# Local attention of both heads of a tile together, and three longer distances in the recurrence's order

## The chip, the cores and the metric

The kernel runs on one core of a Trainium2 chip. The metric is the device time of one execution in microseconds (us). In the text PE is TensorE (its weight loads are shown apart, as PEld), DVE is VectorE, ACT is ScalarE, POOL is GpSimd and SP is SyncE, which here only starts transfers. L517 is line 517 of the kernel.

## What is computed

One layer of a hybrid decoder for 256 prompt tokens and 8 samples of 8 tokens each, 320 columns in all, at model width 2048:

```
xn = RMSNorm(x);  p = xn @ w_in            # 82 tiles of 128 columns
A: RWKV-7 time mixing, 12 heads x 64: per token  S = S*w + sa (kk*a)^T + v k^T,  o = S r
B: sliding-window attention (window 128), 12 query heads on 4 key/value heads, 64 wide,
   softmax with a learned sink per head; the samples also see 128 cached keys each
C: cross-attention, 4 heads x 128, into 256 memory tokens
merged = sum_i sigmoid(gate_i) * (o_i @ w_br_i);  h = x + RMSNorm(merged @ w_o)
y = h + RMSNorm((gelu(conv3(z_gate)) * z_val) @ w_ffn_down)
```

All data are 32-bit floats. Branch B is what the change reorders, and in branch A three places of its order.

## The kernel before, in words

**The weight stream.** Every large product is made with split operands: a weight chunk of up to 8 tiles is loaded by SP, ACT rounds it to its upper part (`wh`, L356 or L96) and DVE subtracts to get the lower part (`wl`, L357 or L97); each weight tile then meets 320 columns in a group of three matmuls (L101 to L103). All activations are kept transposed, features on partitions and tokens in columns.

**The planner.** In the recurrence and the attention PE's order is written out while the program is built, by `pump`: a clock counts 0.405 for each group of three matmuls of the job queue; threads (Python generators) hand in their small operations between groups and give with `yield d` the distance until they go on, or a condition to wait for. PE runs exactly this order; the order on DVE, ACT and POOL is chosen by the tile framework's scheduler, and semaphores keep what depends on what. A distance that is too short shows as a wait on PE.

**The recurrence** (about 88 to 545 us) treats the 12 heads as 6 pairs `hp`. The job queue holds for each pair the projections k, r, v (16 groups each) and then 2 or 3 filler jobs (q, k, v of the attention, 16 groups each); after these come the 16 gate jobs. A job's `done` (L447 to L456) shifts the tokens of its result on POOL, ACT and DVE. `allearly` runs `early(hp)` for one pair after another; its places on PE are, in order:

- L493, the decay and a projections;
- 1.5 behind k: the scaled key `kk` and its square on ACT (L505, L506), and at once the norm matmul L517, which sums the squares; DVE follows with L518 to L524;
- behind r: `ar` and `bk` on DVE (L529 to L533), and 4.0 later the scores L543; here the thread `inverse(hp)` starts, whose first DVE operations (L620, L621) stand 6.0 later and need a round trip by DMA (`sc`, then `NI`);
- 2.0 later the transposes L566 and L572 (of `ar`), with copies by DVE and ACT (L578, L583);
- 1.5 behind v: the transposes of v, again L572, with eight copies into AU by DVE and ACT in turns (L593);
- `TRS` = 2.4 later the 20 products L600, their copy L601, and the bonus matmul L603.

`inverse(hp)` and `late(hp)` (the state's chain and the output) run as threads of their own, about one pair behind. The PSUM banks of `early` and of the tail of `late` come from one pool of two (`pea`).

**The attention** (about 550 to 800 us) runs two threads between groups of the remaining gate and branch jobs: one goes through the memory attention of the prompt (`mem_prompt`, 4 heads) and then through the 6 tiles of the local attention (`swa_prompt`), the other through the memory attention of the samples (`mem_sample`) and then their local attention (`swa_sample`, 2 tiles x 2 groups of 4 samples). A tile has two query heads, one on partitions 0 to 63, the other on 64 to 127. Before, they are done one after the other: scores (two matmuls, 64 rows by 128 columns of the array, 128 and 256 columns streamed), softmax on DVE and ACT (`sink_softmax`), `SSOFT` = 6.0 later three transposes (L869) and their copy (L872), `TRN` = 2.0 later the values (L985, L986: 128 rows by 64 columns). For the samples the scores of one head are four strips of 32 columns (L1005, L1007). Scores and transposes take their PSUM banks from a pool of 3 (`smp1`), the accumulators from a pool of 2 for the prompt and 1 for the samples (`accp`).

Of the kernel before, what the change touches and what calls it, by code (L numbers as in the profile page):

```python
# [9 lines left out]
F32 = mybir.dt.float32  # L10
# [4 lines left out]
PSUM = bass.MemoryType.PSUM  # L15

T = 320
TP = 256
# [11 lines left out]
E0 = 9.0  # L30
TRS = 2.4
NRM = (4, 3, 2)
# [6 lines left out]
SOFT = 3.5  # L39
SSOFT = 6.0  # L40
TRN = 2.0
# [21 lines left out]
def tile_hybrid_step(ctx: ExitStack, tc: tile.TileContext, i, o):  # L63
    nc = tc.nc
    V, A, G, PE = nc.vector, nc.scalar, nc.gpsimd, nc.tensor
# [84 lines left out]
    def split(h, l, src):  # L150
        A.copy(out=h, in_=src)  # L151
        V.tensor_sub(out=l, in0=src, in1=h.bitcast(F32))
# [10 lines left out]
    mv = ap.tile([128, 2, 512], F32, tag="mv", name="mv")  # L163
    QKV = ap.tile([128, 10, T], F32, tag="QKV", name="QKV")
# [3 lines left out]
    with tc.tile_pool(name="st", bufs=1, side="right") as st, tc.tile_pool(name="st2", bufs=3, side="right") as st2, \  # L168
# [122 lines left out]
        sm = spread(smp, smt, 1, tbs=TB[:2])  # L291
# [42 lines left out]
    clock = [0.0]  # L334
# [71 lines left out]
    with tc.tile_pool(name="rws", bufs=1, side="right") as rws, tc.tile_pool(name="rwp", bufs=2, side="right") as rwp, \  # L406
# [31 lines left out]
        def tt():  # L438
            return rwt.tile([128, T], F32, tag="t", name="rt")
# [47 lines left out]
        def early(hp):  # L487
# [17 lines left out]
            A.activation(out=kk, in_=sk, func=AF.Copy, scale=col("kk", hp))  # L505
            A.activation(out=sq, in_=kk, func=AF.Square)  # L506
            eLe, eL = x1, tt()
            A.activation(out=eLe, in_=x1, func=AF.Exp, scale=-C2)
            A.activation(out=eL, in_=L, func=AF.Exp, scale=-C2)
            emL = L  # L510
            A.activation(out=emL, in_=L, func=AF.Exp, scale=C2)
            yield lambda: state["late"] >= hp - 1
            pc = rwm.tile([128, 16], F32, tag="pc", name="pc")
# [72 lines left out]
            sv = rkv[hp, "v"]  # L586
            yield 1.5
            ps1 = pea.tile([128, 512], F32, tag="sm", name="sm")
            turned(ps1, sv)
            for q in range(4):  # L590
                for h in range(2):
                    ng = 3 if q < 2 else 2
                    (A.copy if h else V.tensor_copy)(out=AU[64 * h + 32:64 * h + 64, q:min(4 * ng, 10):4, 64:128],  # L593
                                                     in_=ps1[32 * q:32 * q + 32, 0:128 * ng].rearrange("p (g f) -> p g f", f=128)[:, :, fss[h]])
            yield TRS
            ps1 = pea.tile([128, 512], F32, tag="sm", name="sm").rearrange("p (c t) -> p c t", t=64)
# [217 lines left out]
    with tc.tile_pool(name="at", bufs=1, side="right") as at, tc.tile_pool(name="at2", bufs=2, side="right") as at2, \  # L814
            tc.tile_pool(name="smp1", bufs=3, space=PSUM) as smp, tc.tile_pool(name="accp", bufs=2, space=PSUM) as accp, \
            tc.manual_schedule(engines=MANUAL):
# [61 lines left out]
        def mem_unit(h, qb, pso):  # L878
            pss = smp.tile([128, 512], F32, tag="sm", name="sm")
            PE.matmul(pss[:, 0:256], MQ[:, h, 128 * qb:128 * qb + 128], mkT[:, h, :], start=True, stop=True)  # L880
            pr = softmax(pss[:, 0:256], 256, MS, "p")
            yield SOFT
            pt = transposed(pr, ((0, 128), (128, 128)), "p")
            yield TRN
            for kb in range(2):
                PE.matmul(pso[:, 128 * qb:128 * qb + 128], mv[:, kb, 128 * h:128 * h + 128],
                          pt[:, 128 * kb:128 * kb + 128], start=kb == 0, stop=kb == 1)

        def mem_prompt(h):
            pso = accp.tile([128, 512], F32, tag="acc", name="pso")  # L890
            for qb in range(2):
                yield from mem_unit(h, qb, pso)
            split(OMH[:, h, 0:TP], OML[:, h, 0:TP], pso[:, 0:TP])
            state["om"] += 1

        def mem_sample():
            for b in range(8):
                bg, s = b // 4, b % 4
                if s == 0:
                    po = accp.tile([128, 512], F32, tag="accs", name="psos", bufs=1)  # L900
                ck = at2.tile([128, 4, 256], F32, tag="ck", name="ck")
# [49 lines left out]
        def sink_softmax(src, mask, n, sinkcol, blocks, th):  # L951
# [16 lines left out]
            return pr  # L968

        def swa_prompt(ti):  # L970
            pso = accp.tile([128, 512], F32, tag="acc", name="pso")
            for r in range(2):
                rs = slice(64 * r, 64 * r + 64)
                n = 2 * (ti // 3) + r
                head = 3 * n + ti % 3
                kt = 6 + ti // 3
                pss = smp.tile([128, 512], F32, tag="sm", name="sm")
                PE.matmul(pss[:, 0:128], QKV[rs, ti, 0:128], QKV[rs, kt, 0:128], start=True, stop=True)
                PE.matmul(pss[:, 128:384], QKV[rs, ti, 128:256], QKV[rs, kt, 0:256], start=True, stop=True)
                pr = sink_softmax(pss[:, 0:384], amask[:, 0:384], 384, snk[:, head:head + 1], ((0, 128), (128, 384)), "p")  # L980
                yield SSOFT
                pt = transposed(pr, ((0, 128), (128, 128), (256, 128)), "p")
                yield TRN
                vd = slice(64 * n, 64 * n + 64)
                PE.matmul(pso[rs, 0:256], Vt[:, 0, vd], pt[:, 0:256], start=True, stop=False)  # L985
                PE.matmul(pso[rs, 128:256], Vt[:, 1, vd], pt[:, 256:384], start=False, stop=True)  # L986
            split(OSH[:, ti, 0:TP], OSL[:, ti, 0:TP], pso[:, 0:TP])
            state["os"] += 1

        def swa_sample(n2):  # L990
            for bg in range(2):
                po = accp.tile([128, 512], F32, tag="accs", name="psos", bufs=1)
                ck = at2.tile([128, 4, 128], F32, tag="ck", name="sck")
# [3 lines left out]
                yield 4.0  # L997
                for r in range(2):
                    rs = slice(64 * r, 64 * r + 64)
                    n = 2 * n2 + r  # L1000
                    pss = smp.tile([128, 512], F32, tag="sm", name="sm")
                    for s in range(4):
                        b = 4 * bg + s
                        q = QS[rs, n2, b, :]
                        PE.matmul(pss[32 * s:32 * s + 32, 0:128], q, ck[rs, s, :], start=True, stop=True,  # L1005
                                  tile_position=(64 * r, 32 * s))
                        PE.matmul(pss[32 * s:32 * s + 32, 128:192], q, QKV[rs, 6 + n2, TP:T], start=True, stop=True,  # L1007
                                  tile_position=(64 * r, 32 * s))
                    pr = sink_softmax(pss[:, 0:192], amask[:, 384 + 192 * bg:576 + 192 * bg], 192, snk[:, 12 + n:13 + n], ((0, 192),), "s")
                    yield SSOFT  # L1010
                    pt = transposed(pr, ((0, 128), (128, 64)), "s")
                    yield TRN
                    vd = slice(64 * r, 64 * r + 64)
                    PE.matmul(po[:, vd], pt[0:64, 128:256], Vn[:, 64 * n:64 * n + 64], start=True, stop=False)
                    for s in range(4):
                        PE.matmul(po[32 * s:32 * s + 32, vd], pt[:, 32 * s:32 * s + 32], cv[:, s, vd], start=False, stop=True,
                                  tile_position=(0, 32 * s))
                ob = at2.tile([128, 128], F32, tag="ob", name="ob")
# [340 lines left out]
```

## Time and profile before

| | |
|---|---|
| median of 3 runs | 2075.04 us (2074.26 to 2076.94) |
| profiled execution: its own time | 2076.5 us |
| profiled execution: span, first to last instruction | 2074.7 us |
| granted PE clock, mean over the span | 0.987 |
| busy: PE, DVE, ACT, POOL | 97%, 59%, 40%, 10% |
| memory traffic, mean | 146 GB/s |

The clock is that of PE in shares of full speed (2.4 GHz; the other level is 1.2 GHz, shown as 0.50). A matmul of 32-bit floats that are not rounded leaves two records. An "idle" time stands with what ended it: `[2.24 <-ACT rt L506]` means that the engine waited 2.24 us and that ACT's operation at L506 on tile `rt` released it. A span of a merged row is from the start of its first record to the end of its last.

### The profile page before, as it was taken

Reading aid. Unit: us, or ns where it says so; the run is one execution under the profiler, and the core shown is the slowest. Engines: PE = TensorE matmul, PEld = TensorE weight load, DVE = VectorE, ACT = ScalarE, POOL = GpSimd, SP = SyncE. Lnnn points to the kernel's source line nnn. Section 1 sums busy time; section 2 is a strip of 40 time slices with the busy share of each in tenths; the row PEclk is TensorE's granted clock in tenths of the full one; section 3 lists DMA queues with packets and bytes.
Section 4 is the critical chain, followed back from the end, with each engine's and each line's share of the span. In section 5 each row is a group of like instructions: output and inputs, shape, how many; then the busy total and the mean of one; then the engine's idle time right before and its main releaser. Section 6 shows DMA issues by size and latency. Waiting matters only on the chain.

```text
span 2074.7 us, 36358 instructions
## 1 busy us (share of the span) xinstructions
PE 2009.7 (97%) x14875; PEld 1940.3 (94%) x14875; DVE 1234.4 (59%) x2048; ACT 823.3 (40%) x1306; POOL 197.7 (10%) x452
## 2 busy tenths in 40 slices
PE   8899898989999999999999999999999999999997
PEld 7788797889998899999999999999999999999997
DVE  7778778885456764444546753555555555455456
ACT  5534343343333443333445443343333333334335
POOL 4511221021200000000100100000000000000001
PEclk9999899999999999999999999999999999999998
DMA  7443333334545334544543344445444444444444
GB/s 272 160 126 96 113 114 96 93 119 127 181 170 160 114 122 142 163 152 150 191 173 132 129 152 146 150 153 187 147 151 152 148 148 152 153 148 147 153 138 125
DMA packets 93000, 303.28 MB, mean 146 GB/s; under 512 B 11356, under 2 KB 17654, under 8 KB 92816
## 3 DMA queue, kind: packets, MB, share of 16 engines
q1 hardware_dynamic: 83232, 273.42, 39.7%
q0 software_dynamic: 8880, 26.71, 4.0%
q8 instruction: 117, 1.92, 0.4%
q10 hardware_dynamic: 720, 0.82, 0.1%
q14 instruction: 51, 0.42, 0.1%
HBM read 293.53 MB, written 9.34 MB: 146 GB/s over the span
## 4 chain that ended last, share of the span: by engine, by line
PE 84%; issue 6%; DVE 5%; DMA 2%; ACT 1%; POOL 1%; SPq 0%; POOLq 0%; DVEq 0%; ACTq 0%
PE bigps L101 25%; PE bigps L102 25%; PE bigps L103 24%; DMA NI<-sc 1%; DVE wl L357 1%; ACT wh L356 1%; DMA sc<-BT 0%; PE bigps L1130 0%; DVE wl L217 0%; PE sm L869 0%; PE sm L493 0%; PE bigps L1128 0%; PE bigps L1131 0%; PE sm L701 0%; PE sm L146 0%
## 5 line engine op out<-in xcount | busy, mean ns | idle before, releaser
L101 PE MATMUL bigps<-XH,wh 128*128 128x320 f32 x2656 | 846.3, 319 | 0.5 <-ACT mv L319 0.5
L103 PE MATMUL bigps<-XH,wl 128*128 128x320 f32 x2656 | 826.7, 311 | 2.1 <-DVE wl L357 2.1
L102 PE MATMUL bigps<-XL,wh 128*128 128x320 f32 x2656 | 827.0, 311 | 1.6 <-POOL XL L257 1.5
L101 PEld LDWEIGHTS bigps<-XH,wh 128*128 128x128 f32 x2656 | 504.5, 190 | 18.9 <-issue 14.8
L97 DVE TENSOR_TENSOR wl<-raw,wh 128x1024 fp32r<-128x1024 f32 (+1 forms) x299 | 357.4, 1196 | 274.7 <-ACT wh L96 273.9
L96 ACT CAST wh<-raw 128x1024 fp32r<-128x1024 f32 (+1 forms) x299 | 306.4, 1025 | 519.4 <-PE bigps L102 396.6
L102 PEld LDWEIGHTS bigps<-XL,wh 128*128 128x128 f32 x2656 | 504.5, 190 | 4.3 <-POOL XL L257 2.4
L103 PEld LDWEIGHTS bigps<-XH,wl 128*128 128x128 f32 x2656 | 503.9, 190 | 2.6 <-DVE wl L357 2.6
L357 DVE TENSOR_TENSOR wl<-raw,wh 128x1024 fp32r<-128x1024 f32 (+2 forms) x212 | 245.4, 1158 | 190.1 <-ACT wh L356 189.9
L356 ACT CAST wh<-raw 128x1024 fp32r<-128x1024 f32 (+2 forms) x212 | 208.4, 983 | 313.6 <-PE bigps L102 262.7
L102 PE MATMUL bigps<-fl,wh 128*128 128x320 f32 x704 | 217.5, 309 | 0.0
L101 PE MATMUL bigps<-fh,wh 128*128 128x320 f32 x704 | 217.4, 309 | 0.0
L103 PE MATMUL bigps<-fh,wl 128*128 128x320 f32 x704 | 217.4, 309 | 0.0
L101 PEld LDWEIGHTS bigps<-fh,wh 128*128 128x128 f32 x704 | 132.2, 188 | 0.2 <-ACT fh L151 0.2
L102 PEld LDWEIGHTS bigps<-fl,wh 128*128 128x128 f32 x704 | 132.2, 188 | 0.1
L103 PEld LDWEIGHTS bigps<-fh,wl 128*128 128x128 f32 x704 | 132.2, 188 | 0.0
L1187 DVE TENSOR_TENSOR yacc<-yacc,bigps 128x320 f32<-128x320 f32 x80 | 38.9, 487 | 84.4 <-PE bigps L103 84.2
L1161 POOL COPY cout<-zp 128x9 f32<-128x9 f32 x88 | 16.8, 221 | 732.4 <-DVE zp L1158 732.4
L101 PE MATMUL bigps<-MG,wh 128*128 128x320 f32 x208 | 64.4, 309 | 0.3 <-ACT MG L811 0.3
L103 PE MATMUL bigps<-MG,wl 128*128 128x320 f32 x208 | 64.3, 309 | 0.0
L102 PE MATMUL bigps<-MG,wh 128*128 128x320 f32 x208 | 64.3, 309 | 0.0
L1157 DVE TENSOR_TENSOR zp<-bigps,S 128x256 f32<-128x256 f32 x44 | 18.7, 425 | 57.1 <-PE bigps L103 57.1
(406 smaller groups left out, 2393.5 us busy)
## 6 DMA issues: line engine op xcount, KB each, us to landing
raw<-in_wup SPq DMA_DIRECT2D x176, 512.0 KB, 3.6
raw<-in_win SPq DMA_DIRECT2D x164, 512.0 KB, 3.6
raw<-in_wdn SPq DMA_DIRECT2D x80, 512.0 KB, 3.2
raw<-in_wo SPq DMA_DIRECT2D x32, 512.0 KB, 3.8
raw<-in_wbr_rw SPq DMA_DIRECT2D x16, 384.0 KB, 3.2
raw<-in_wbr_sw SPq DMA_DIRECT2D x16, 384.0 KB, 3.2
ck<-in_cmk POOLq DMA_DIRECT2D x8, 512.0 KB, 4.8
cv<-in_cmv POOLq DMA_DIRECT2D x8, 512.0 KB, 3.8
```

The source lines that it names most:

```text
L96: A.copy(out=h, in_=raw)
L97: V.tensor_sub(out=l, in0=raw, in1=h.bitcast(F32))
L101: PE.matmul(ps, h, xh, start=start, stop=False)
L102: PE.matmul(ps, h, xl, start=False, stop=False)
L103: PE.matmul(ps, l, xh, start=False, stop=stop)
L356: A.copy(out=h, in_=c[2])
L357: V.tensor_sub(out=l, in0=c[2], in1=h.bitcast(F32))
L1157: V.tensor_mul(out=zp[:, 2:258], in0=psz[:, 0:TP], in1=S2[:, 0:TP])
L1161: G.tensor_copy(out=cout[:, j, :, e], in_=zp[:, 256 + e:337 + e:10])
L1187: V.tensor_add(out=yacc[:, m, :], in0=yacc[:, m, :], in1=ps)
```

## The change

Three distances in `early`: the norm matmul stands at least `KKN` = 3.2 behind the operations on ACT that it needs (before: at once); the turning of v stands `TRN_V` = 3.6 behind v (before 1.5); the products stand `PRE` = 4.8 behind the turning (before 2.4).

In the local attention both heads of a tile are done together. For the prompt the scores of one head and block of keys are two matmuls of 64 query columns each in place of one of 128, issued so that they alternate between the four 64 x 64 quarters of the array; each head has its own PSUM bank. Then come both softmaxes, `SSOFT2` = 9.0 later the transposes of both, `TRN2` = 3.6 later the values of both, on the two column halves. For the samples the strips of both heads alternate in the same way, and the transposes and values of both stand together. `smp1` gets 4 banks, `accp` 1 and 1; the accumulator of the prompt is asked for just ahead of the first values matmul.

```
-TRS = 2.4
+KKN, TRN_V, PRE = 3.2, 3.6, 4.8
-SSOFT = 6.0
+SSOFT2, TRN2 = 9.0, 3.6
...
             A.activation(out=sq, in_=kk, func=AF.Square)
+            ready = clock[0] + KKN
...
-            yield lambda: state["late"] >= hp - 1
+            yield lambda: state["late"] >= hp - 1 and clock[0] >= ready
...
             sv = rkv[hp, "v"]
-            yield 1.5
+            yield TRN_V
...
-            yield TRS
+            yield PRE
...
-            tc.tile_pool(name="smp1", bufs=3, space=PSUM) as smp, tc.tile_pool(name="accp", bufs=2, space=PSUM) as accp, \
+            tc.tile_pool(name="smp1", bufs=4, space=PSUM) as smp, tc.tile_pool(name="accp", bufs=1, space=PSUM) as accp, \
...
         def swa_prompt(ti):
+            kt = 6 + ti // 3
+            pss = [smp.tile([128, 512], F32, tag="sm", name="sm") for _ in range(2)]
+            for lo, hi, q0, k1 in ((0, 128, 0, 128), (128, 384, 128, 256)):
+                for c in range(2):
+                    for r, rs in enumerate(halves2):
+                        qs = slice(64 * (c ^ r), 64 * (c ^ r) + 64)
+                        PE.matmul(pss[r][qs, lo:hi], QKV[rs, ti, q0 + qs.start:q0 + qs.stop], QKV[rs, kt, 0:k1], start=True, stop=True)
+            prs = []
+            for r in range(2):
+                head = 6 * (ti // 3) + 3 * r + ti % 3
+                prs.append(sink_softmax(pss[r][:, 0:384], amask[:, 0:384], 384, snk[:, head:head + 1], ((0, 128), (128, 384)), "p"))
+            yield SSOFT2
+            pts = [transposed(pr, ((0, 128), (128, 128), (256, 128)), "p") for pr in prs]
+            yield TRN2
             pso = accp.tile([128, 512], F32, tag="acc", name="pso")
...
+            for r, rs in enumerate(halves2):
+                PE.matmul(pso[rs, 0:256], Vt[:, 0, vd[r]], pts[r][:, 0:256], start=True, stop=False)
+            for r, rs in enumerate(halves2):
+                PE.matmul(pso[rs, 128:256], Vt[:, 1, vd[r]], pts[r][:, 256:384], start=False, stop=True)
...
         def swa_sample(n2):
...
+                pss = [smp.tile([128, 512], F32, tag="sm", name="sm") for _ in range(2)]
+                for s in range(4):
+                    for r, rs in enumerate(halves2):
+                        q = QS[rs, n2, 4 * bg + s, :]
+                        PE.matmul(pss[r][32 * s:32 * s + 32, 0:128], q, ck[rs, s, :], start=True, stop=True,
+                                  tile_position=(64 * r, 32 * s))
+                        PE.matmul(pss[r][32 * s:32 * s + 32, 128:192], q, QKV[rs, 6 + n2, TP:T], start=True, stop=True,
+                                  tile_position=(64 * r, 32 * s))
+                prs = [sink_softmax(pss[r][:, 0:192], ...) for r in range(2)]
+                yield SSOFT2
+                pts = [transposed(pr, ((0, 128), (128, 64)), "s") for pr in prs]
+                yield TRN2
...
```

## Rows read from the trace of the kernel before

**Rows 1.** The page, part 1: busy time of PE, share of the span and instructions.

```profile
PE 2009.7 (97%) x14875; PEld 1940.3 (94%) x14875; DVE 1234.4 (59%) x2048; ACT 823.3 (40%) x1306; POOL 197.7 (10%) x452
```

**Rows 2.** Windows by stage: length, PE, PEld, DVE, ACT, POOL busy, PE clock, DMA share, GB/s.

```profile
100.00:500.00 400.00, 367.91 (x3409) 336.21 (x3408) 309.73 (x568) 155.08 (x315) 72.38 (x140) 0.95 0.36 108
...
553.00:800.00 247.00, 246.37 (x1888) 222.81 (x1887) 154.71 (x384) 95.61 (x218) 18.17 (x33) 1.00 0.48 153
```

**Rows 3.** Waits of PE: total us, times, longest us.

```profile
PE sm L517 <- ACT rt L506: 10.6, 5, 2.3
PE sm L600 <- DVE AU L593: 9.7, 8, 1.8
PE sm L572 <- DVE rkv L454: 9.4, 6, 1.6
```

**Rows 4.** PE's timeline (start, length), two groups at each clock; one window.

```profile
252.00 0.47 PE L101 MATMUL bigps<-XH,wh 128*128 128x320 f32 x1
...
252.80 0.47 PE L101 MATMUL bigps<-XH,wh 128*128 128x320 f32 x1
...
254.89 0.31 PE L101 MATMUL bigps<-XH,wh 128*128 128x320 f32 x1
...
255.33 0.31 PE L101 MATMUL bigps<-XH,wh 128*128 128x320 f32 x1
...
244.00:255.00 11.00, 10.22 (x56) 8.06 (x57) 8.97 (x20) 2.37 (x5) 0.00 (x0) 0.53 0.15 48
```

**Rows 5.** PE's timeline, places of the first head pair.

```profile
97.83 0.81 PE L517 MATMUL sm<-rt,cst 128*128 128x320 f32 x2 [2.24 <-ACT rt L506]
...
108.24 1.38 PE L543 MATMUL sm<-ar,bk 64*64 64x64 f32 x40
...
116.67 0.78 PE L572 MATMUL sm<-cst,rkv 128*128 128x128 f32 x3 [1.58 <-DVE rkv L454]
...
123.19 0.92 PE L600 MATMUL sm<-AU,BT 32*32 32x64 f32 x28 [1.23 <-DVE AU L593]
```

**Rows 6.** DVE: a window, the splits L357 in it, the timeline's L532.

```profile
98.60:107.30 8.70, 8.38 (x14) 1.00 0.23 72
...
98.60:107.30 8.70, 2.44 (x2) 1.00 0.23 72
...
106.75 0.49 DVE L532 TENSOR_TENSOR ar<-rkv,rt 128x320 f32<-128x320 f32 x1
```

**Rows 7.** DVE's timeline among the copies into AU.

```profile
119.81 0.17 DVE L620 TENSOR_TENSOR prod<-rcst,NI 120x4 f32<-120x4 f32 x1 [1.14 <-DMA NI<-sc]
...
122.85 0.29 DVE L593 COPY AU<-sm 32x128 f32<-32x128 f32 x1
```

**Rows 8.** PE's timeline, one prompt head's values and the next scores.

```profile
631.51 0.31 PE L103 MATMUL bigps<-ORH,wl 128*128 128x320 f32 x1
631.75 0.65 PE L985 MATMUL pso<-pt,Vt 128*64 128x256 f32 x2
...
632.55 0.48 PE L978 MATMUL sm<-QKV 64*128 64x128 f32 x2
...
633.40 0.41 PE L101 MATMUL bigps<-ORH,wh 128*128 128x320 f32 x1
```

**Rows 9.** PE's timeline, one sample head's values and the next scores.

```profile
689.94 0.43 PE L1014 MATMUL psos<-Vn,pt 64*128 64x64 f32 x2
...
691.03 0.41 PE L101 MATMUL bigps<-OMH,wh 128*128 128x320 f32 x1
```

**Rows 10.** PE's timeline, four column strips of the memory attention's values.

```profile
577.93 0.64 PE L917 MATMUL psos<-cv,pt 128*32 128x128 f32 x16
578.50 0.71 PE L886 MATMUL pso<-pt,mv 128*128 128x128 f32 x4
```

**Rows 11.** DVE's timeline, first and last operation of one sample softmax.

```profile
691.72 0.35 DVE L953 TENSOR_TENSOR pr<-sm,amask 128x192 f32<-128x192 f32 x1
...
696.83 0.31 DVE L967 TENSOR_SCALAR pr<-pr,stat 128x192 f32<-128x192 f32 x1
```

More of the change, by code (lines that the diff above doesn't have):

```diff
@@ L884, in mem_unit @@
             yield TRN
+            if qb == 0:
+                pso.append(accp.tile([128, 512], F32, tag="acc", name="pso"))
             for kb in range(2):
-                PE.matmul(pso[:, 128 * qb:128 * qb + 128], mv[:, kb, 128 * h:128 * h + 128],
+                PE.matmul(pso[0][:, 128 * qb:128 * qb + 128], mv[:, kb, 128 * h:128 * h + 128],
                           pt[:, 128 * kb:128 * kb + 128], start=kb == 0, stop=kb == 1)
         def mem_prompt(h):
-            pso = accp.tile([128, 512], F32, tag="acc", name="pso")
+            pso = []
             for qb in range(2):
                 yield from mem_unit(h, qb, pso)
-            split(OMH[:, h, 0:TP], OML[:, h, 0:TP], pso[:, 0:TP])
+            split(OMH[:, h, 0:TP], OML[:, h, 0:TP], pso[0][:, 0:TP])
             state["om"] += 1
@@ L899, in mem_sample @@
                 if s == 0:
-                    po = accp.tile([128, 512], F32, tag="accs", name="psos", bufs=1)
+                    po = accp.tile([128, 512], F32, tag="accs", name="psos")
                 ck = at2.tile([128, 4, 256], F32, tag="ck", name="ck")
@@ L968, in sink_softmax @@
             return pr
+        halves2 = [slice(64 * r, 64 * r + 64) for r in range(2)]
         def swa_prompt(ti):
-            pso = accp.tile([128, 512], F32, tag="acc", name="pso")
[L972 to L986, printed above, removed]
+            kt = 6 + ti // 3
[12 more added lines that the diff above has]
+            yield TRN2
+            pso = accp.tile([128, 512], F32, tag="acc", name="pso")
+            vd = [slice(64 * (2 * (ti // 3) + r), 64 * (2 * (ti // 3) + r) + 64) for r in range(2)]
+            for r, rs in enumerate(halves2):
+                PE.matmul(pso[rs, 0:256], Vt[:, 0, vd[r]], pts[r][:, 0:256], start=True, stop=False)
+            for r, rs in enumerate(halves2):
+                PE.matmul(pso[rs, 128:256], Vt[:, 1, vd[r]], pts[r][:, 256:384], start=False, stop=True)
@@ L991, in swa_sample @@
             for bg in range(2):
-                po = accp.tile([128, 512], F32, tag="accs", name="psos", bufs=1)
+                po = accp.tile([128, 512], F32, tag="accs", name="psos")
                 ck = at2.tile([128, 4, 128], F32, tag="ck", name="sck")
@@ L997, in swa_sample @@
                 yield 4.0
[L998 to L1001, printed above, removed]
-                    for s in range(4):
[L1003 to L1017, printed above, removed]
@@ new lines, in swa_sample @@
+                prs = [sink_softmax(pss[r][:, 0:192], amask[:, 384 + 192 * bg:576 + 192 * bg], 192,
+                                    snk[:, 12 + 2 * n2 + r:13 + 2 * n2 + r], ((0, 192),), "s") for r in range(2)]
+                yield SSOFT2
+                pts = [transposed(pr, ((0, 128), (128, 64)), "s") for pr in prs]
+                yield TRN2
+                for r, rs in enumerate(halves2):
+                    PE.matmul(po[:, rs], pts[r][0:64, 128:256], Vn[:, 128 * n2 + 64 * r:128 * n2 + 64 * r + 64], start=r == 0, stop=False,
+                              skip_group_check=True)
@@ L1018, in swa_sample @@
+                for r, rs in enumerate(halves2):
+                    for s in range(4):
+                        PE.matmul(po[32 * s:32 * s + 32, rs], pts[r][:, 32 * s:32 * s + 32], cv[:, s, rs], start=False, stop=True,
+                                  tile_position=(0, 32 * s), skip_group_check=True)
                 ob = at2.tile([128, 128], F32, tag="ob", name="ob")
```

## The prediction, made before the changed kernel was run

> **What bounds the kernel now.** I read the page's busy shares first, then the windows by stage, then the list of waits of TensorE (PE), and last the timelines of PE and VectorE (DVE) around each wait.
>
> PE is busy for 97% of the span [rows 1], so the time is PE's work plus its gaps. The windows say where the gaps are: from 100 to 500 us (the recurrence) PE works 367.9 of 400 us at a mean granted clock of 0.95; from 553 to 800 us (the attention) it works 246.4 of 247 us at full clock [rows 2]. So the recurrence can be shortened by taking gaps away, and the attention only by giving PE less to do. The three largest waits there are the ones that the three distances concern: the norm matmul L517 behind the square on ScalarE (ACT), 10.6 us; the products L600 behind the copies into AU, 9.7 us; the turning of v, L572, behind its token shift, 9.4 us [rows 3]. Together 29.7 us.
>
> Part of the lost time is clock. At full clock one group of three matmuls of the weight stream takes 0.44 us, at the lower of the two levels 0.80 us [rows 4], so 45% of such time is lost. A mean clock of 0.95 over 400 us is 40 us at half clock [rows 2], worth at most 40 x 0.45 = 18 us (less, as some of it is waiting). The drop from 244 to 255 us follows the waits of one L600 [rows 4]; but after the 2.24 us wait for the first L517 [rows 5] the clock stayed at 1.00 [rows 6], so not every wait costs clock.
>
> **The change, part by part.** The planner's clock counts 0.405 per group, so a distance is a number of groups of 0.44 us: 1.5 is 4 groups, 2.4 is 6, 3.2 is 8, 3.6 is 9, 4.0 is 10, 4.8 is 12. Weight jobs are always there to fill them: after v come 2 or 3 filler jobs of 16 groups, and the longer path behind v takes 9 + 12 = 21 groups (before 4 + 6). So the distances themselves cost nothing; their order of work stays, and they issue no DMA.
>
> *Turning of v (1.5 to 3.6).* The first L572 on v stands at 116.67 us after 1.58 us of waiting and 4 groups (1.76 us) [rows 5]: v's last matmul was over at 113.33 and its shift was ready 3.34 us later. Nine groups are 3.96 us, 0.6 us to spare, in all six head pairs alike. Gain 9.4 us; I take 9, bounds 6 (if the shift is late behind a weight split on DVE) and 9.4.
>
> *Norm matmul (KKN).* k was over at 97.83 - 2.24 - 1.76 = 93.83 us; the square is ready 4.0 us later [rows 5], and the new place, 4 + 8 = 12 groups behind k, is 5.3 us later. L517's wait goes. But what is late next is the scores matmul L543. It keeps its place, 10 groups behind r, and r is 16 groups behind k: with about 0.7 of the norm matmul's own 0.81 us that is 26 x 0.44 + 0.7 = 12.1 us after k, at 105.9. From L517's start to the end of L532, the last DVE operation that the scores need, it is 107.24 - 97.83 = 9.4 us, and DVE worked 8.4 of 8.7 us there, two weight splits of together 2.4 us among it [rows 6]. Started at 99.1 this chain ends at 108.5, or at 107.3 if one of the two splits now falls ahead of it. The wait of 2.24 us comes back as one of 1.4 to 2.6 us in front of the scores. In the later head pairs the tail of the pair before adds DVE work and some PE work to the same stretch. Bounds for the six together: 10.6 us gained (DVE's order changes so that the chain fits) to 5 lost (2.6 six times). I take a gain of 3, about the lower wait in each pair.
>
> *Products (TRS 2.4 to PRE 4.8).* L600's last inputs came at 123.19 us, 9.86 us behind v [rows 5]; 21 groups and the turning's 0.55 us put it at 9.8. If the copies stayed where they are, the wait would be gone. They do not quite: they come from the turning, now 0.6 us later, and DVE runs in order. Already before, the copies stood in DVE's queue behind L620, which waited 1.14 us for the DMA that brings NI; the last DVE copy was issued at 122.85, 3.0 us after it [rows 7]. With the copies issued later, more of them fall behind that DMA. So between nothing gained and all 9.7; I take 5, as half of each wait is then covered.
>
> *Clock.* With some 17 of 30 us of waits gone I take 8 of the 18 us; bounds 0 and 18.
>
> *Prompt attention.* For one head PE now runs L985, L986 (values) and then L978, L979 (scores of the next head). The last weight matmul starts at 631.51 and takes 0.15, the next starts at 633.40: 1.74 us per head, of which the scores are 0.85 and the values 0.80 [rows 8]. Two heads per tile make 3.48 us. In the change the values of both heads stand on two column halves next to each other, and the scores on four quarters. If those run at once, a tile costs what a head did: gain 6 x 1.74 = 10.4 us. That halves run at once the trace shows: the 20 scores matmuls of the recurrence, each of 64 columns on one of two diagonal quarters, take 1.38 us [rows 5], while at 0.85 us per 384 columns in a row they would be 2.8. Four quarters at once, two of them in the same columns, stand nowhere in the trace. Bounds for the scores: 0.85 per tile (four at once), 1.70 (two at once, as now), 3.40 (one by one).
>
> *Column halves that share all rows* are the one point where a page speaks against the change. The row: eight matmuls on four column strips, all 128 rows, take 0.57 us until the next group starts [rows 10]; by the 0.85 us per 384 columns they would be 2.3 us in a row. The Trainium skill, "TensorE: Matmul & The Clock Gate", Part 3, "The mechanism", says that a weight load overlaps matmuls in flight only where the row group differs; by that the value halves would run in turn. The trace disagrees by a factor of four, so I keep the gain, and give the rule a small chance below.
>
> *Sample attention.* One head takes from about 689.85 to 691.03, 1.18 us [rows 9], 8 heads. Together, the scores of two (0.48 us, eight strips) may cost one, the two L1014 then stand next to each other, and L1016 gains nothing (both heads on the same strips): about 0.8 us per pair, 3.3 us in all; bounds 0 and 4.7.
>
> *Waits in the attention.* The distances per pair (9.0 and 3.6: 23 and 9 groups, 10.1 and 4.0 us) replace two of 6.0 and 2.0. One sample unit took from 691.72 to 697.14 between its first and last DVE operation while the other thread's unit ran too [rows 11]. The second head runs behind the first on DVE and ACT, so a pair needs between 5.4 and 10.8 us; nearest to the lower end plus one unit's own DVE work (some 2.5 us), 8 us, inside 10.1. I set 1.7 us aside for waits, so the attention gives 10.4 + 3.3 - 1.7 = 12 us. The single accumulator bank is asked for only at the values, 12.6 clock units after the last split, and costs nothing.
>
> **Sum** against the profiled execution (2076.5 us, span 2074.7): 9 + 3 + 5 + 8 + 12 = 37 us less, 2039.5. That execution lies 1.5 us above the median of the runs shown (2075.0), so the forecast is 2038.
>
> **Rivals.**
> *The waits form again on DVE* (25%). For it: 8.4 of 8.7 us in rows 6, and the queue in rows 7. Against it: one of the two splits can fall ahead of L517. L572's 9 and the attention's 12 stay, L600 gives 0, the norm loses 3 (2.3 in each pair), the clock nothing: 18 us less, 2057.
> *All waits and all slow clock go* (12%). For it: the covers counted in groups suffice at L572 and L600. Against it: the scores' chain. 14 + 30 + 18 = 62 us less, 2013.
> *The quarters do not run four at once* (8%), so that the change does not do what it says. Nothing in the trace has two row halves in the same columns together. Two at once: 0.85 x 6 + 0.48 x 4 = 7 us of the gain go, 2045; one by one: another 10, 2055.
> *Column halves in turn* (3%): 0.80 x 6 = 4.8 us of the gain go, 2043. This is what the rule of "TensorE: Matmul & The Clock Gate" in the Trainium skill gives here; rows 10 speak against it.
> *The pair's softmax is late at the transposes L869: slower than before* (6%). If both chains run one after the other at 5.4 us and are held up by the splits, 10.8 us and more meet 10.1. What such a wait costs in clock is open: none after the 2.24 us before the first L517, but 11 us x 0.47 x 2 x 0.45 = 4.6 us from 244 on, behind a wait of at most 1.8 us [rows 3, 4]; half of that is 2.3. There are 10 pairs; to eat 37 us each must lose 3.7 us, that is a wait of 1.4 us with its clock. At 2 us it is 10 x 4.3 = 43: 2081. Against it: L869 is not among the large waits now [rows 3], and DVE is 63% busy there (154.7 of 247 us) [rows 2]. The Trainium skill, "TensorEngine Tiling (Array Packing)", "PSUM Bottleneck", states the same danger: tiling speeds up TensorE and not the engines that empty PSUM; no run yet shows it here.
>
> **How the numbers follow.** Forecast 46%, with its own range 2026 to 2052. The range 2014 to 2062 takes in the second, fourth and fifth cases and half of the third; about 2 in 10 is left out, on the low side of "all go", on the slower side, and in sums of the bounds. A difference of 0.2% (4 us) is about what a measurement can tell. Faster by more: 0.91 (everything but the slow rival and sums of bad bounds); within: 0.04; slower: 0.05.
>
> **What would show it.** In the trace of the changed kernel: L572 without waits; L517 without, and L543 with waits of 1 to 2.5 us behind DVE; L600 with waits under 1 us; PE's clock from 100 to 460 us above 0.96; the gap in the weight stream at a tile's values and the next one's scores 1.7 to 1.9 us, once per tile, and the waits at L869 under 0.5 us each. The forecast is wrong if the quarters take over 1.3 us per tile, if L543 stays free of waits and the clock at 1.00, or if L869 waits by microseconds.

## The result, and the profile of the changed kernel

The changed kernel takes 2053.36 us (median of 4 runs, 2050.91 to 2054.78) against 2075.99 us (4 runs of the kernel before beside it): a ratio of 0.9886, 95% interval 0.9871 to 0.9902, some 23 us less. The forecast was 2038, its range 2014 to 2062: faster as forecast, by about 60% of the amount. The profiled execution took 2050.9 us, 25.6 less than that of before.

Below, the recurrence is the stretch on PE from the first L493 to the last matmul of `late` (L763 before, L764 after); what follows it holds the gates, the attention and the feed-forward. The change moves most lines of the recurrence by one (L517 is now L518, L543 L544, L572 L573, L600 L601) and the local attention's further (scores L982, values L993 and L995, transposes L870).

| profiled execution | before | after | forecast |
|---|---|---|---|
| recurrence, us | 460.3 | 448.0 (-12.3) | -25 |
| from there to the end, us | 1525.5 | 1512.4 (-13.1) | -12 |
| waits of PE in the recurrence, us | 33.8 | 28.5 | -17 |
| half-clock time in it, us | 41.0 | 41.0 | clock gains 8 |

(Half-clock time is (1 - granted clock) x 2, summed over windows of 1 us.) The profiled execution of after is the shortest of its four, so the timed difference of 23 us is the safer one. The attention gave what was asked and the recurrence about half.

The page's part 1 of after, and its two windows by stage, to set beside [rows 1, 2]:

```profile
PE 1988.0 (97%) x14923; PEld 1929.5 (94%) x14923; DVE 1226.4 (60%) x2048; ACT 821.6 (40%) x1306; POOL 203.1 (10%) x452
...
100.00:500.00 400.00, 371.12 (x3489) 343.11 (x3488) 314.10 (x577) 157.82 (x322) 78.97 (x140) 0.95 0.37 113
553.00:800.00 247.00, 244.94 (x2011) 228.88 (x2011) 153.09 (x384) 99.14 (x218) 11.78 (x19) 1.00 0.47 150
```

From 100 to 500 us PE is busy for 3 us more and the clock is still 0.95. The attention is again a stage without gaps: it became shorter because PE has less to do.

The waits of PE from 88 to 545 us, after (us, times, longest), beside [rows 3]:

```profile
PE sm L493 <- DVE AP L602: 13.9, 5, 3.8
PE sm L146 <- DVE rex L138: 6.0, 4, 4.2
PE sm L689 <- ACT AU L674: 1.9, 2, 1.7
PE sm L764 <- DVE rp L760: 1.9, 1, 1.9
PE sm L493 <- ACT rt L495: 1.2, 2, 0.6
PE sm L601 <- ACT AU L594: 1.2, 2, 0.6
...
PE sm L601 <- DVE AU L594: 0.7, 3, 0.3
```

The three waits of [rows 3] are gone: L518 and L573 are not in the list, L601 has 1.9 us left. New at the top is **L493, 15.1 us**, which the prediction did not name. It is the first matmul pair of the next `early`, and it needs both banks of `pea`: those that the products and the bonus have just filled, and that VectorE's L602 and L607 empty. PE's timeline of the first head pair, after, beside [rows 5]:

```profile
98.81 0.70 PE L518 MATMUL sm<-rt,cst 128*128 128x320 f32 x2
106.05 1.38 PE L544 MATMUL sm<-ar,bk 64*64 64x64 f32 x40 [0.38 <-DVE ar L533]
114.93 0.49 PE L573 MATMUL sm<-cst,rkv 128*128 128x128 f32 x3
122.33 0.63 PE L601 MATMUL sm<-AU,BT 32*32 32x64 f32 x26 [0.58 <-ACT AU L594]
125.73 2.09 PE L493 MATMUL sm<-lora,lw 64*128 64x320 f32 x4 [2.04 <-DVE AP L602]
```

And VectorE's timeline around that copy, beside [rows 7]:

```profile
119.73 0.17 DVE L621 TENSOR_TENSOR prod<-rcst,NI 120x4 f32<-120x4 f32 x1 [1.98 <-DMA NI<-sc]
...
125.19 0.49 DVE L602 COPY AP<-sm 128x320 f32<-128x320 f32 x1
```

The products' main run starts at 122.33 and ends before the bonus matmul at 122.89; the copy that empties their bank is issued 2.3 us later, because L621 and L622 of the inverse, started late by the transfer, and a weight split (L357 at 122.47, 1.22 us) stand ahead of it in VectorE's queue. L493 pays 2.04 us.

The stage of the attention: PE at one prompt tile, and at one pair of sample heads' scores, beside [rows 8, 9]; then the only large wait at the transposes.

```profile
625.92 0.30 PE L103 MATMUL bigps<-ORH,wl 128*128 128x320 f32 x1
626.15 0.65 PE L993 MATMUL pso<-pt,Vt 128*64 128x256 f32 x4
626.64 0.39 PE L995 MATMUL pso<-pt,Vt 128*64 128x128 f32 x4
626.96 0.88 PE L982 MATMUL sm<-QKV 64*64 64x128 f32 x16
627.77 0.42 PE L101 MATMUL bigps<-ORH,wh 128*128 128x320 f32 x1
...
691.66 0.50 PE L1011 MATMUL sm<-sck,QS 64*32 64x128 f32 x16
691.90 0.36 PE L1013 MATMUL sm<-QKV,QS 64*32 64x64 f32 x16
692.20 0.41 PE L101 MATMUL bigps<-XH,wh 128*128 128x320 f32 x1
...
652.84 0.41 PE L870 MATMUL sm<-cst,pr 128*128 128x128 f32 x2 [1.36 <-DVE pr L864]
```

The scores of both heads take 0.81 us (626.96 to 627.77), the values of both 0.81: what one head took before. The scores of a sample pair take 0.54.

### The profile page after: what moved, and what is told of

The parts are those of the page before. It is cut to its first block, busy times and chain, and to the rows that moved or that the text cites. A ratio compares the mean times of both kernels' runs of the same rounds, so it can differ in the third digit from the quotient of the medians.

```text
span 2049.1 us, 36434 instructions
## 1 busy us (share of the span) xinstructions
PE 1988.0 (97%) x14923; PEld 1929.5 (94%) x14923; DVE 1226.4 (60%) x2048; ACT 821.6 (40%) x1306; POOL 203.1 (10%) x452
## 4 chain that ended last, share of the span: by engine, by line
PE 60%; issue 5%; POOL 1%; DVE 0%; ACT 0%; POOLq 0%; DVEq 0%
PE bigps L101 19%; PE bigps L102 19%; PE bigps L103 19%; PE bigps L1139 0%; PE bigps L1137 0%; PE bigps L1140 0%; POOL yacc L1227 0%; POOL merged L1062 0%; POOL yacc L1228 0%; DVE MG L813 0%; PE sm L146 0%; PE sm L870 0%; POOL rsr L1087 0%; PE psos L1021 0%; PE sm L1212 0%
## 5 line engine op out<-in xcount | busy, mean ns | idle before, releaser
L357 DVE TENSOR_TENSOR wl<-raw,wh 128x1024 fp32r<-128x1024 f32 (+2 forms) x212 | 245.2, 1157 | 197.4 <-ACT wh L356 193.8
```

Of the source, the lines that this page charges most:

```text
L357: V.tensor_sub(out=l, in0=c[2], in1=h.bitcast(F32))
```

## The experiments

Ratios are to runs of the kernel before on the same chip, with 95% intervals; a difference of 0.001 is 2.1 us. The waits and half-clock times are of one profiled execution each. All later kernels have the new attention, and their time from the recurrence's end to the end of the span is 1512.3 to 1514.3 us, so what they differ by lies in the recurrence.

**e1, e2: the two halves of the change alone.** e1 has the three distances and the old attention, e2 the new attention and the old distances:

```diff
-KKN, TRN_V, PRE = 3.2, 3.6, 4.8
+KKN, TRN_V, PRE = 0.0, 1.5, 2.4     # e2
```

> The kernel before with the three distances alone, the attention as it was. Theory: in the changed kernel's trace the last L740 of the recurrence starts 12.5 us earlier (522.73 against 535.21 us), so the distances alone give 12.5 us (about 2063 against 2076), with 13 to 16 us of waits at L493 behind the copy into AP. Rival: the distances give nothing and the attention all of the 22.6 us: within 4 us of the kernel before. Rival 2, from the forecast: 25 us, 2051.

> The changed kernel with the three distances at their old values, so the attention alone. Theory: 13 us less than before (forecast 12), about 2063, with the waits of before at L518 (10.6 us), L601 (10) and L573 (9.4) and almost none at L493. Rival: the attention gives only half (quarters two at once, forecast 2045 of 2038, that is 5 to 7 us): 2069 to 2071.

e1: 2066.40 us, 0.9937 (0.9916 to 0.9958), 13 us less; e2: 2063.99 us, 0.9928 (0.9909 to 0.9948), 15 us less. Both theories held. In e2 the recurrence takes 463.0 us with 36.2 us of waits (before 460.3 and 33.8), and the rest 1512.4; in e1 the rest is 1525.6. The parts are separate and add up within their intervals (13 + 15 against 23). The attention is settled; the missing gain is in the distances.

**e3: room ahead of L493.**

```diff
-            yield E0 if hp == 0 else 0.0
+            yield E0 if hp == 0 else 4.8
```

> The changed kernel; the two matmuls L493 of the next head pair stand 4.8 (12 groups) behind the bonus matmul in place of at once. Theory: PE stands at L493 only because both banks of its pool still hold the products and the bonus, which DVE copies out late behind the inverse's operations; with weight groups in between, the 15.1 us of waits at L493 fall under 3 and the kernel gains 12 to 18 us on the changed one (about 2038). Rival: DVE is the bound of the recurrence (78% busy there); then the waits come again at L518, L544 or L146 and the time stays within 5 us of 2053.

2048.76 us, 0.9856 (0.9828 to 0.9883): in time the rival held. L493 no longer waits, yet the waits sum to 28.8 us as in after (28.5):

```profile
PE sm L146 <- DVE rex L138: 8.2, 3, 4.0
PE psb L724 <- ACT SA L726: 6.2, 3, 2.1
PE sm L129 <- ACT rp L754: 3.4, 1, 3.4
```

They went on to the state's chain and the output of `late`. What fell in the profiled execution is the half-clock time, from 41.0 to 27.3 us. That is not so in all four: the two at a granted clock of 0.990 and 0.989 took 2046.1 and 2043.9 us, the two at 0.985 took 2054.7 and 2051.4, which is after's clock and time. The interval overlaps that of after.

**e4: the products back at 2.4.**

```diff
-KKN, TRN_V, PRE = 3.2, 3.6, 4.8
+KKN, TRN_V, PRE = 3.2, 3.6, 2.4
```

> The changed kernel with PRE back at 2.4, KKN and TRN_V as changed. Theory: it is the longer distance ahead of the products that pushes their copy behind the inverse's operations on DVE; with 2.4 the waits at L493 fall from 15 to under 5 us and those at L601 rise from 2 to 6 to 10 us, and the time stays within 5 us of the changed kernel's 2053. Rival: the waits at L493 come from the later turning of v, which 2.4 does not undo: L493 keeps 10 us or more and L601 comes on top, 2058 or more.

2064.17 us, 0.9927 (0.9905 to 0.9948): all of the distances' gain is gone. The theory had the direction of the waits right (L493 falls to 0.3 us, L601 rises to 13.4) and the time wrong; the rival had a time in its range, but not L493. The sum of waits is *smaller* than in after (25.9 us), but 68.3 us of the profiled execution run at half clock. So a sum of waits doesn't price them.

**e5: less work on VectorE.** The inverse leaves out its sums over earlier blocks (L631, L633, L635 for blocks 1 to 3):

```diff
-                w = E[0:120, :, 0:8]
-                if b:
...
-                    V.tensor_add(out=w, in0=w, in1=E[0:120, :, nj:nj + 8])
+                w = E[0:120, :, 8 * b:8 * b + 8]
```

> The changed kernel with work left out of the inverse: for blocks 1 to 3 the products of earlier blocks (L631, L633, L635, some 48 us on VectorE in the recurrence) are not computed. Nothing is taken from TensorE, ScalarE or the transfers, and all distances stay. Theory (VectorE's work and its order bound the recurrence, so waits only change place when a distance changes): the waits of TensorE in the recurrence, 28 us in the changed kernel, fall under 15, those at L493 under 7, and the time falls by 12 to 25 us, to 2030 to 2041. Rival (the waits are a matter of the planner's distances alone): L493 keeps 12 us or more, time within 4 us of 2053.

2051.07 us, 0.9878 (0.9863 to 0.9893). The same window in after and in e5:

```profile
88.00:530.00 442.00, 413.08 (x3901) 382.25 (x3900) 333.57 (x605) 177.13 (x358) 84.70 (x152) 0.95 0.37 113
```

```profile
88.00:530.00 442.00, 418.66 (x3893) 388.13 (x3893) 282.03 (x527) 177.42 (x358) 86.46 (x152) 0.93 0.37 113
```

VectorE has 52 us less to do and the time moves by 2, within the intervals: its throughput is not the bound, and in time the rival held. L493 still waits 10.4 us. The waits of PE do fall, to 23.1 us, but this execution ran 58.0 us at half clock (after 41.0).

**e6: no norm distance.**

```diff
-KKN, TRN_V, PRE = 3.2, 3.6, 4.8
+KKN, TRN_V, PRE = 0.0, 3.6, 4.8
```

> The changed kernel with KKN back at 0: the norm matmul at once, TRN_V and PRE as changed. Theory: L518's 10.6 us of waits come back; the 6 us at L146 and 2 us at L764, which came because the norm's chain on VectorE now meets the tail of the pair before, go; L493 keeps about 14: KKN is worth 2 to 5 us, 2055 to 2058. Rival, the forecast's price: its gain is given back at the scores, 3 us, and nothing changes at L146. Rival 2: all 10.6 us and their clock, 2064 or more.

2050.56 us, 0.9872 (0.9857 to 0.9887). L518 waits its 10.1 us again, and L146 (now 1.1), L764 (0.6) and L493 (10.7) give back as much: 26.3 us in all. The theory had L146 and L764 right, but theory and rivals all wanted more time. The distance on which the prediction set 3 us saves nothing.

**e7: scores on row halves.** Each head's scores are two matmuls of 128 query columns again, with the two heads in turn:

```diff
-                for c in range(2):
-                    for r, rs in enumerate(halves2):
...
+                for r, rs in enumerate(halves2):
+                    PE.matmul(pss[r][:, lo:hi], QKV[rs, ti, q0:q0 + 128], QKV[rs, kt, 0:k1], start=True, stop=True)
```

> The changed kernel with the prompt's scores not cut into quarters: per head and block of keys one matmul of 128 query columns, the two heads alternating, on the two row halves and all columns, each head in its own bank. Theory: row halves run at once too, so a tile's scores take 0.8 to 0.9 us as with quarters (0.81) and the time stays within 3 us of 2053: what gains is that both heads stand together, not the quarters. Rival: matmuls that share columns run in turn; then 1.6 to 1.7 us per tile, 5 us more, 2058.

2053.04 us, 0.9885 (0.9870 to 0.9900): after's time, as the theory had it. PE at the same tile:

```profile
626.95 0.93 PE L980 MATMUL sm<-QKV 64*128 64x128 f32 x8
627.81 0.41 PE L101 MATMUL bigps<-ORH,wh 128*128 128x320 f32 x1
```

0.86 us for both heads against 0.81 on quarters. The gain is from two heads side by side on the rows; cutting the columns in two saves another 0.05 us per tile.

**e8: the copies of `early` and the state's into AU on ScalarE,** at L579, L584, L594, L602 and L674.

```diff
-                    (A.copy if h else V.tensor_copy)(out=AU[64 * h + 32:64 * h + 64, ...
+                    A.copy(out=AU[64 * h + 32:64 * h + 64, ...
...
-            V.tensor_copy(out=AP[:, :, 64:128], in_=ps1[:, 0:5])
+            A.copy(out=AP[:, :, 64:128], in_=ps1[:, 0:5])
```

> The changed kernel with copies of the recurrence moved from VectorE to ScalarE: those of L579, L584, L594, L674 that VectorE had, and L602, the copy into AP (about 27 us off VectorE, whose share there is 78%, onto ScalarE, 39%). Theory: the copy into AP no longer stands behind the inverse's operations, the waits at L493 fall from 15 to under 5 us, and the time falls by 8 to 16 us (2038 to 2045). Rival: the pairs of copies that VectorE and ScalarE shared now run one after the other on ScalarE behind its casts, and waits at L601, L689 and L573 grow by as much: 2050 or more.

2050.35 us, 0.9868 (0.9852 to 0.9885), overlapping after. The theory missed; the rival had the time, but of its waits only L573's grew (to 2.4 us). The wait at L493 (16.1 us in all) only changes its releaser:

```profile
PE sm L493 <- DVE bonus L607: 13.9, 5, 3.7
```

The other bank is the bonus's, still emptied by VectorE. Both banks must come free, so moving one of the two copies is worth nothing there.

**e9, e10: one distance alone,** the turning's and the products'.

```diff
-KKN, TRN_V, PRE = 3.2, 3.6, 4.8
+KKN, TRN_V, PRE = 0.0, 3.6, 2.4     # e9
+KKN, TRN_V, PRE = 0.0, 1.5, 4.8     # e10
```

> Both-heads attention kept; of the three distances only the turning of v is longer (TRN_V 3.6; KKN 0, PRE 2.4). Theory: of the distances it is the one ahead of the products (PRE) that pays, since without it (e4) the time was 10.8 us above the changed kernel and equal to that with none of the three (e2, 2064 us). Then this kernel, too, takes 2062 to 2067 us: L573's 9.4 us of waits are gone, but L601's come back as 12 to 15 us with the lower clock behind them. Rival: in e4 the longer norm distance did the harm, and the turning alone is worth its 9.4 us: 2053 to 2057 us.

> Both-heads attention kept; only the distance ahead of the products is longer (PRE 4.8; KKN 0, TRN_V 1.5). Theory: it carries the gain of the three; 2051 to 2057 us, although L573 waits its 9 us again. Rival: the turning and the products pay only together, since the copies into AU start from the turning and the 9.4 us of waits at L573 are real lost time: 2058 to 2064 us.

e9: 2053.9 us, 0.9876 (0.9863 to 0.9890); e10: 2063.34 us, 0.9935 (0.9922 to 0.9947). My theory, that the products' distance pays, fell in both; the rivals held in time. But what e10's rival gave as its reason, that the turning and the products pay only together, did not hold: e9 has the gain without the products. The distances with the new attention, by the runs (waits and half-clock time in us):

| KKN, TRN_V, PRE | run | ratio | waits | at half clock |
|---|---|---|---|---|
| 0, 1.5, 2.4 | e2 | 0.9928 | 36.2 | 41.0 |
| 0, 1.5, 4.8 | e10 | 0.9935 | 34.5 | 41.0 |
| 0, 3.6, 2.4 | e9 | 0.9876 | 22.0 | 47.8 |
| 0, 3.6, 4.8 | e6 | 0.9872 | 26.3 | 44.4 |
| 3.2, 3.6, 2.4 | e4 | 0.9927 | 25.9 | 68.3 |
| 3.2, 3.6, 4.8 | after | 0.9886 | 28.5 | 41.0 |

The turning alone is worth 0.0052, 10.8 us. The products' distance is worth nothing where the norm's is absent (e10 against e2, e6 against e9). The norm's distance, put behind the turning's alone, *costs* 0.0051, 10.6 us (e4 against e9, intervals apart); with the products' distance as well its price shrinks to 3 us, within the intervals (after against e6). So in the change `PRE` mostly repairs what `KKN` breaks. (`KKN` by itself was not run.)

What `KKN` breaks can be followed in the third head pair. e4 first: PE's timeline (one row), VectorE's (one), POOL's (three), VectorE's (one), PE's (two).

```profile
234.46 1.38 PE L544 MATMUL sm<-ar,bk 64*64 64x64 f32 x40
...
237.07 0.87 DVE L547 TENSOR_TENSOR BT<-sm,cst 128x512 f32<-128x512 f32 x2
...
238.24 1.21 POOL L557 DMA_DIRECT2D sc<-BT  x2 [2.64 <-DVE BT L547]
241.79 0.19 POOL L452 COPY shout<-pad 128x9 f32<-128x9 f32 x1 [2.35 <-ACT pad L450]
243.31 0.62 POOL L559 DMA_DIRECT2D NI<-sc  x1 [1.32 <-DMA sc<-BT]
...
250.06 0.17 DVE L621 TENSOR_TENSOR prod<-rcst,NI 120x4 f32<-120x4 f32 x1 [3.88 <-DMA NI<-sc]
...
246.41 0.46 PE L601 MATMUL sm<-AU,BT 32*32 32x64 f32 x8
251.01 2.11 PE L601 MATMUL sm<-AU,BT 32*32 32x64 f32 x32 [4.14 <-DVE AU L594]
```

The same places in e9:

```profile
232.07 1.38 PE L544 MATMUL sm<-ar,bk 64*64 64x64 f32 x40
...
233.37 0.88 DVE L547 TENSOR_TENSOR BT<-sm,cst 128x512 f32<-128x512 f32 x2
...
234.55 1.26 POOL L557 DMA_DIRECT2D sc<-BT  x2 [3.04 <-DVE BT L547]
238.48 0.62 POOL L559 DMA_DIRECT2D NI<-sc  x1 [2.67 <-DMA sc<-BT]
239.40 0.19 POOL L452 COPY shout<-pad 128x9 f32<-128x9 f32 x1 [0.30 <-ACT pad L450]
...
243.86 0.17 DVE L621 TENSOR_TENSOR prod<-rcst,NI 120x4 f32<-120x4 f32 x1
...
244.02 0.46 PE L601 MATMUL sm<-AU,BT 32*32 32x64 f32 x8
```

In both kernels the first product stands 11.95 us behind the first of the scores L544 (246.41 and 244.02). The inverse's round trip starts from the same scores. From L544 to the use of NI at L621 it is 15.6 us in e4 and at most 11.8 in e9, so without `KKN` it fits ahead of the products and with `KKN` it doesn't. Three parts make the difference:

- The masking L547, which fills BT for the transfer, starts 2.61 us behind L544 in e4 and 1.30 in e9: with `KKN` two weight splits L357 (234.33 and 235.93) stand between VectorE's L533 and L547, without it one.
- From the first transfer's issue to the second's it is 5.07 us in e4 and 3.93 in e9.
- From there to the use of NI it is 6.75 and at most 5.38.

With `KKN` the token shift's copy L452 stands ahead of the second transfer L559 in POOL's queue; without it L452 stands behind. That order is not what costs here: L452 is over at 241.98, and POOL then waits another 1.32 us for the first transfer to land. In after and e4 such a wait of 0.7 to 1.3 us follows L452 each time that it stands there. So it is the transfers themselves that took longer. While the second was under way the core moved 223 GB/s in e4 (243.3 to 250.0 us) and 165 in e9 (238.5 to 243.84); no run varied that by itself, and for the first transfer the cause stays open (158 against 175 GB/s).

VectorE sits in front of L621 until NI lands, with the last two copies into AU behind it, and the products wait for those (4.14 us). In after the round trip takes as long (15.8 us in the third pair), but `PRE` puts the products 16.1 us behind the scores. Summed over the six pairs VectorE waits 11.3 us for NI in e4 and 2.6 in e9; by the same view 9.5 in after, 13.2 in e1, 10.0 in e3, 9.8 in e8 (all with `KKN`), and 2.6 in e6 and 3.0 in e11 (without). The turning's distance has a part in it: at 1.5 and without `KKN` it is 6.1 in before, 8.4 in e2 and 5.5 in e10.

**e11, e12: the best of these together.** e12 adds e8's copies to e11:

```diff
-KKN, TRN_V, PRE = 3.2, 3.6, 4.8
+KKN, TRN_V, PRE = 0.0, 3.6, 4.8
...
-            yield E0 if hp == 0 else 0.0
+            yield E0 if hp == 0 else 4.8
```

> The changed kernel with 4.8 ahead of L493 (as e3) and without the norm distance (as e6). Theory: each of the two gave 3 to 5 us by another wait (L493's 15 us, and L146 and L764); if what they save adds up, 2045 to 2049 us. Rival: the waits are handed on as before, and the time stays at 2049 to 2053 us with a sum of waits of 25 to 30 us.

> e11 and all the copies out of PSUM in early (BT, AP, AU, and L602) on ScalarE, as in e8. Theory: VectorE's in-order queue is what the handed-on waits have in common (L493, L146, L601, L702); with the copies off it the sum of waits falls under 20 us and the time to 2040 to 2046 us. Rival: ScalarE's own queue (exponentials, the copies of late) takes its place, or another wait does: 2047 to 2053 us.

e11: **2045.28 us, 0.9841 (0.9828 to 0.9853)**, the fastest kernel here, 9 us below after with the intervals apart. e12: 2047.53 us, 0.9855 (0.9842 to 0.9868), with 29.5 us of waits: its rival held. The largest waits of e11:

```profile
PE sm L518 <- ACT rt L506: 13.3, 6, 4.7
PE sm L129 <- ACT rp L754: 5.6, 2, 3.8
PE psb L724 <- ACT SA L726: 4.1, 3, 2.1
```

The theory's time held. The waits are 27.2 us, about as many as in after (28.5). But none stands at the products or at L493, and 34.1 us are at half clock; the granted clock is 0.988 to 0.992 in the four executions, in after's four 0.984 to 0.987. In e12 the waits at L724 behind ScalarE grow to 9.1 us: the copies' load is handed to the other engine's queue.

## Why the prediction was half right

**Turning of v (forecast 9 us): right.** L573 on v waits no more in after, and e9 measures 10.8 us for it alone. It is a wait of PE for a token shift, and nine groups cover it. That 10.8 lies so near to 9 is partly luck: from e2 to e9 L601's waits fall too, from 11.9 to 5.0 us, which the term did not count, and the half-clock time rises by 7 us.

**Norm matmul (forecast 3, bounds -5 to 10.6): the step that failed.** The prediction expected L518's wait to come back at the scores as 1.4 to 2.6 us per pair. L544 waits only 1.5 us in all: in the first pair one weight split came ahead of the norm's operations and one behind L533, as VectorE's timeline of after shows, so the chain ended at 105.99 and not at 107.3:

```profile
98.96 1.23 DVE L357 TENSOR_TENSOR wl<-raw,wh 128x1024 fp32r<-128x1024 f32 x1 [1.31 <-PE bigps L103]
100.10 0.49 DVE L519 TENSOR_SCALAR sm<-sm 128x320 f32<-128x320 f32 x1
...
105.50 0.49 DVE L533 TENSOR_TENSOR ar<-rkv,rt 128x320 f32<-128x320 f32 x1
105.91 1.22 DVE L357 TENSOR_TENSOR wl<-raw,wh 128x1024 fp32r<-128x1024 f32 x1
```

What the step left out is the round trip of NI, which runs from the same scores to the same copies into AU. The prediction counted that trip for the products only, and held that the distances by themselves cost nothing; but `KKN` changed the order on VectorE, and the trip grew from at most 11.8 to 15.6 us (third pair, e9 and e4), past the products' 11.95. e6 prices `KKN` at -3 us (within the intervals), e4 against e9 at -10.6.

**Products (forecast 5, "half of each wait is covered"): the wait went, the gain did not.** L600's 9.9 us (9.7 of them behind DVE) fell to 1.9 at L601. But the step asked only who is late *for* the products, not who waits *behind* them: L493 needs their bank and the bonus's, and its waits grew to 15.1 us. e10 shows the exchange without the other distances: L601's 11.9 us of e2 fall to 0.2, L493 takes 8.4 instead of 0.9, and the sum hardly moves (36.2 to 34.5 us), nor does the time.

**Clock (forecast 8): nothing.** It followed from 17 us of waits going; 5.3 went (33.8 to 28.5). By the windows most stretches at half clock lie where they lay, at the products and L493. Three of them in after:

```profile
124.00:132.00 8.00, 6.27 (x22) 5.24 (x23) 6.68 (x14) 2.47 (x4) 0.00 (x0) 0.57 0.19 66
244.00:255.00 11.00, 7.72 (x25) 5.44 (x27) 8.98 (x18) 4.14 (x8) 0.00 (x0) 0.53 0.17 49
319.00:330.00 11.00, 11.00 (x125) 10.07 (x126) 7.42 (x16) 2.54 (x5) 0.00 (x0) 0.53 0.02 9
```

244 to 255 us is the very window of [rows 4], at the same clock, with PE busy for 2.5 us less.

**Prompt and sample attention (forecast 12): right, 13.1.** The gap per tile was forecast as 1.7 to 1.9 us; counted as there (0.15 us behind the start of the last weight matmul, 625.92, to 627.77) it is 1.70. The column halves do not run in turn. The Trainium skill, "TensorE: Matmul & The Clock Gate", Part 3, "The mechanism", says that a weight load overlaps matmuls in flight only where the row group differs. The trace disagrees with that rule: the values of both heads share all rows and still take 0.81 us together, where one head took 0.80 [rows 8]. The slower rival did not come: L870 waited once, 1.36 us, and the 1.7 us set aside for waits are about what was paid.

**The rivals.** "The waits form again on DVE" (25%, 2057 us) came nearest in its mechanism: its place was wrong (L493 and L146, not L543 and L600), and e5 shows that it isn't VectorE's load that makes them; at L493 the trace shows what stands ahead of the copy in VectorE's queue. The quarters one by one (2055 us) are nearer in number, but the scores' 0.81 us per tile rules them out. What was wrong in size is thus the sum 3 + 5 + 8 of the norm, the products and the clock: 16 us forecast, 12.3 - 9.4 = 3 us found in the profiled pair. That the time still lies in the range is owed to the range's width and to the two terms that were right.

**What stays open.** The sum of waits and the half-clock time do not follow each other (e9: 22.0 and 47.8; e10: 34.5 and 41.0), and executions differ: e1 and after have the same code up to the end of the recurrence, but 455.1 and 448.0 us of it, with 51.2 and 41.0 us at half clock. Of differences of 3 us, as of e6 or e8 against after, nothing is said.

## What to carry to other kernels

Before a distance is lengthened to cover a wait, list who needs the buffers that the moved work holds, and which in-order queues and which round trips by DMA its helpers share: the wait reappears there, and its sum may not change at all. Lengthen one distance at a time and time each: here one of three carried the gain, one did nothing by itself, and one cost 10.6 us until another repaired it. Two small matmul sets on disjoint rows or disjoint columns of the array are worth pairing even where the scheduling around them gets coarser.

## What the runs showed of the hardware that was not expected

- Two heads' scores in unrounded 32-bit floats, each on 64 rows and all 128 columns of the array, took 0.86 us where one head's took 0.85 [rows 8]; on four 64 x 64 quarters 0.81.
- In one kernel the time followed the granted clock: e3's executions at 0.990 and 0.989 took 2046.1 and 2043.9 us, those at 0.985 2054.7 and 2051.4.
- A wait is not priced by its length. e4's waits sum to 25.9 us and after's to 28.5, but e4's profiled execution ran 27 us more at half clock. That pair overstates it: it has the lowest granted clock of e4's four executions (0.978, the others 0.982 to 0.984) and the highest of after's (0.987, the others 0.984 and 0.985). By the means of the four, 0.9815 and 0.985, e4 runs some 15 us more at half clock; at the 45% loss of [rows 4] that is an estimate of 7 us, and the timed difference is 8.5 (0.9927 against 0.9886).
- Waits of the same size cost differently by place. In after 37.5 of the 41 us at half clock lie in five stretches at the products and at L493's 15.1 us of waits, of 3.4 to 10.2 us each, one of them (319 to 330 us) with PE busy throughout. e11's 13.3 us at L518 have three stretches of together 10 us behind them, and a fourth of 6.8 that they share with a wait at L129.
- The second transfer of the inverse's round trip took from 4.2 to 7.5 us to land in after, 4.5 to 6.1 in e9. Over its 84 issues in the recurrences of all 14 profiles, the 20 that landed in under 4.8 us did so while the core moved 141 GB/s in the mean, the 18 that took 6 us and more at 202 GB/s. That is a relation, not a cause that was tried.
